# Weight products that stream their tokens in descending order: a hybrid decoder layer on one Trainium2 core

## The chip, the cores and the metric

The kernel runs on 1 core of one Trainium2 chip. The metric is the device time of one execution in microseconds (us), as the median of several runs. A profiled execution of the same kernel gives the trace.

## The reference, cut to what matters

One layer of a decoder for 256 tokens of 2048 features: a modulated RMSNorm, an input projection to three groups of heads (retention, RWKV-7, block-sparse attention), an output projection with a gated residual, then a second modulated norm and a gated MLP with a causal convolution, and a last norm.

```python
def conv_glu_ffn(h, w_up, conv_w, conv_b, w_down):
    S = h.shape[1]
    u = h @ w_up
    up = jnp.pad(u, ((0, 0), (CONV_WIDTH - 1, 0), (0, 0)))
    u = sum(conv_w[j] * up[:, j:j + S] for j in range(CONV_WIDTH)) + conv_b
    val, gate = jnp.split(u, 2, axis=-1)
    return (jax.nn.silu(gate) * val) @ w_down

def reference(x, c, w_in, w_out, ..., norm_final):
    c_act = jax.nn.silu(c)
    for l in range(DEPTH):
        mod = (c_act @ w_ada[l] + b_ada[l])[:, None, :]
        sh1, sc1, g1, sh2, sc2, g2 = jnp.split(mod, 6, axis=-1)
        h = rms_norm(x, norm_mix[l]) * (1.0 + sc1) + sh1
        x = x + g1 * hybrid_mixer(h, w_in[l], w_out[l], ...)
        h = rms_norm(x, norm_ffn[l]) * (1.0 + sc2) + sh2
        x = x + g2 * conv_glu_ffn(h, w_ffn_up[l], ffn_conv_w[l], ffn_conv_b[l], w_ffn_down[l])
    return rms_norm(x, norm_final)
```

The change touches the four large products with the weights: `h @ w_in`, `mixed @ w_out`, `h @ w_up` and the one with `w_down`.

## The kernel before

Activations lie with features on the 128 partitions and the 256 tokens along the free axis. A weight product takes a 128 x 128 block of weights as the stationary operand and a feature slice of 128 x 256 tokens as the moving one, and adds into a 128 x 256 piece of a PSUM bank; an output tile of 128 features is the sum over all feature slices `k`.

To keep fp32 accuracy, weights and activations are each split in a high and a low part of type fp32r (`hi`, `lo`), and three products are made for each block: high by high, high by low, low by high (L1192, L1193, L1194).

The weights stream from memory in blocks of 16 products, 1 MB, in an order that is written out ahead (`ORDER`). A block is turned into two chunks of eight: ScalarE makes the high part (`hi`, L458), VectorE the low part (`lo`, L459). `convert_until` runs `AHEAD` = 2 chunks ahead of TensorE. Among the blocks lie those of the modulation weights (`w_ada`), which VectorE multiplies and sums by itself (`raw`, L413). When one is known, `h_tile` makes one slice of the modulated input: `xn` (L439), `hhi` (L440), `hlo` (L441). Four slices share a tile.

The main loop goes over the chunks. For each of the eight products it opens a piece of a bank if the tile begins, picks the moving operands with `operands` (the tiles `hhi`/`hlo`, `mxhi`/`mxlo` or `ghi`/`glo`), and issues the three matmuls. In the input projection some tiles share a bank in pairs (`both`, tile name `pair`). For the first tiles of the up projection (`early`) the moving operand is `xghi`/`xglo`, 258 columns: 256 tokens and two columns of the shift. A tile whose sum is whole, or stops for a while, goes to `ready` with its piece of the bank and is evacuated by `evac_in`, `evac_out`, `evac_up` or `evac_down` on ScalarE or VectorE (L492, L494, L1032, L1099, L1115, L1133). After each chunk `run_tasks` issues a few steps of the heads, whose matmuls are plain fp32, such as the gate of the RWKV heads (`g`, L680).

Of the kernel before, what the change touches and what calls it, by code (L numbers as in the profile page):

```python
# [173 lines left out]
def trunk(tc, A):  # L174
# [25 lines left out]
    def nm(s):  # L200
        count[0] += 1
        return f"{s}{count[0]}"
# [86 lines left out]
    for f in range(4, NF):  # L289
        part = win[4 if f == 4 else cut[f - 5]:cut[f - 4]]  # L290
# [105 lines left out]
    for g in range(4):  # L396
        ps = psum.tile([128, 512], F32, tag="bg", name=nm("cb"), bufs=4)
# [50 lines left out]
    def convert_until(c):  # L448
        while len(chunks) <= c and pos[0] < len(stream_items):
            it = stream_items[pos[0]]  # L450
            raw = raws[pos[0]]
            if it[0] == "ada":
                ada_block(it[1], it[2], raw[0])
            else:
                half = half_of[0]
                hi, lo = (stream.tile([128, 8, 128], F32R, tag=n, name=nm(n), bufs=CONVB) for n in ("hi", "lo"))
                src = raw[half] if len(raw) == 2 else raw[0][:, 1024 * half:1024 * half + 1024]
                S.copy(flat(hi), src)  # L458
                V.tensor_tensor(flat(lo), src, flat(hi).bitcast(F32), op=OP.subtract)  # L459
                chunks.append((it[1], 16 * it[2] + 8 * half, hi, lo))  # L460
                half_of[0] = 1 - half
                if half_of[0]:
                    continue
            pos[0] += 1
            consumed[0] += 1
            pump()
# [528 lines left out]
    def run_tasks(n):  # L995

        for i in range(n):
            head = first_task[0]
            if head and alive[0] + head[1] <= 3 and (i % 2 == 0 and not hold - finished or not tasks):
                first_task[0] = step(head[0])  # L1000
                continue
            for i, (t, need) in enumerate(tasks):
                if alive[0] + need <= 3:
                    break
            else:
                if head and alive[0] + head[1] <= 3:
                    first_task[0] = step(head[0])
                continue
            tasks.pop(i)
            again = step(t)  # L1010
            if again:
                tasks.append(again)
# [132 lines left out]
    def operands(m, k):  # L1145
        src = H if m in ("in", "up") else MX if m == "out" else GT
        if m == "down":
            k = RANK[k]
        hi, lo = src[k // 4]
        return hi[:, k % 4], lo[:, k % 4]  # L1150
# [15 lines left out]
    for c in range(n_chunks):  # L1166
        convert_until(c + AHEAD)
        for f in hooks.pop(c, []):
            f()
        m, base, whi, wlo = chunks[c]  # L1170
        ready = []
        for j in range(8):
            t, k, first, last, part = ORDER[m][base + j]
            if first:
                spare = c >= first_up
                turn[0] += 1
                if m == "in" and k == 0 and t in S_TILES + W_TILES:

                    if t % 2 == 0:
                        tag, n = ("bg", 4) if t in S_TILES else ("mm", 3) if t != W_TILES[-2] else ("y", 1)  # L1180
                        pair[0] = psum.tile([128, 512], F32, tag=tag, name=nm("pair"), bufs=n)
                    both[t] = pair[0]
                    opened[t] = pair[0][:, T * (t % 2):T * (t % 2) + T]
                elif spare and turn[0] % 2:
                    opened[t] = psum.tile([128, 512], F32, tag="bg", name=nm("mm"), bufs=4)
                else:
                    opened[t] = psum.tile([128, 512], F32, tag="mm", name=nm("mm"), bufs=3)
            early = m == "up" and t % NP < EARLY and k < 4
            ps = opened[t][:, 0:T + 2] if early else opened[t][:, 0:T]
            hi, lo = (x[:, k] for x in XG) if early else operands(m, k)  # L1190
            two = t in both
            PE.matmul(ps, whi[:, j], hi, start=first and not (two and t % 2), stop=False, skip_group_check=two)  # L1192
            PE.matmul(ps, whi[:, j], lo, start=False, stop=False, skip_group_check=two)  # L1193
            PE.matmul(ps, wlo[:, j], hi, start=False, stop=last, skip_group_check=two)  # L1194
            if last:
                del opened[t]
                if not two:
                    ready.append((t, part, ps))
                elif t % 2:
                    ready.append((t - 1, part, both.pop(t)))  # L1200
                    del both[t - 1]
        for t, part, ps in ready:
            evac[m](t, part, ps)
        run_tasks(TASKS)
# [75 lines left out]
```

## Time and profile before

| what | value |
|---|---|
| time, median of 3 runs | 1283.11 us (1282.66 to 1283.84) |
| time of the profiled execution | 1284.61 us |
| span of the profiled execution | 1282.8 us |
| TensorE busy | 1242.3 us, 97% of the span |
| VectorE busy | 1031.6 us, 80% |
| ScalarE busy | 650.6 us, 51% |
| GpSimd busy | 39.9 us, 3% |
| moved from and to memory | 320.56 MB, 250 GB/s in the mean |

The span goes from the first to the last instruction of the trace; the time of the execution is 1.8 us longer. PE is TensorE's matmuls, PEld its weight loads, DVE VectorE, ACT ScalarE, POOL GpSimd. Matmuls are pipelined, so the record of one (some 280 ns) overlaps the next, and the pace is read from start to start.

### The profile page before, as it was taken

What the parts mean: (1) busy time and instruction counts of PE and PEld (TensorE: products, weight loads), DVE (VectorE), ACT (ScalarE), POOL (GpSimd) and SP (SyncE); (2) the same over time, 40 slices, a digit from 0 to 9 for tenths busy, and PEclk for the clock granted to TensorE, in tenths of its full rate; (3) what the DMA queues carried; (4) which work ended last, traced back from release to release, by engine and by line L of the source; (5) the groups of instructions that cost most, each with busy time, mean ns of one, the idle gap of its engine ahead of it and who ended that gap; (6) DMA issues with size and microseconds to landing.
All of it is one profiled execution on the core that took longest, in us unless ns stands there. A gap on an engine that the chain in (4) does not pass through costs nothing.

```text
span 1282.8 us, 25320 instructions
## 1 busy us (share of the span) xinstructions
PE 1242.3 (97%) x10524; PEld 1222.0 (95%) x10524; DVE 1031.6 (80%) x1606; ACT 650.6 (51%) x1043; POOL 39.9 (3%) x41
## 2 busy tenths in 40 slices
PE   5899999999999999999999999999999999999996
PEld 4799999999998999999999999999999999999995
DVE  7988989989988478999896999899866766666444
ACT  4455444665435333566555656666555544444441
POOL 0000000000000000500000000000000000000000
PEclk7999999999999999999999999999999999999998
DMA  9999987786636459867985566565655677777551
GB/s 388 349 360 344 341 311 268 290 294 209 232 104 235 155 204 363 319 233 259 350 307 200 197 213 208 184 225 194 220 205 198 230 263 254 285 254 281 207 197 66
DMA packets 49939, 320.56 MB, mean 250 GB/s; under 512 B 5536, under 2 KB 6048, under 8 KB 15776
## 3 DMA queue, kind: packets, MB, share of 16 engines
q1 hardware_dynamic: 48528, 315.10, 67.8%
q0 software_dynamic: 1008, 3.67, 0.8%
q8 instruction: 82, 1.34, 0.4%
q14 instruction: 33, 0.27, 0.1%
q10 hardware_dynamic: 288, 0.17, 0.0%
HBM read 316.83 MB, written 2.10 MB: 249 GB/s over the span
## 4 chain that ended last, share of the span: by engine, by line
PE 89%; DVE 7%; issue 2%; ACT 1%; DMA 0%; POOL 0%; DVEq 0%; ACTq 0%; POOLq 0%
PE mm L1192 26%; PE mm L1194 26%; PE mm L1193 26%; DVE raw L413 2%; DVE lo L459 2%; PE pair L1194 1%; PE pair L1192 1%; PE pair L1193 1%; PE xx L778 1%; PE u L915 1%; PE sp L923 1%; PE sp L937 1%; PE akv L788 1%; PE yps L917 0%; ACT hi L458 0%
## 5 line engine op out<-in xcount | busy, mean ns | idle before, releaser
L459 DVE TENSOR_TENSOR lo<-raw,hi 128x1024 fp32r<-128x1024 f32 x400 | 488.4, 1224 | 161.0 <-ACT hi L458 158.2
L458 ACT CAST hi<-raw 128x1024 fp32r<-128x1024 f32 x400 | 418.7, 1049 | 391.7 <-PE mm L1193 333.0
L1192 PE MATMUL mm<-hhi,hi 128*128 128x256 f32 x2016 | 560.2, 278 | 0.2
L1194 PE MATMUL mm<-hhi,lo 128*128 128x256 f32 x2016 | 559.4, 278 | 0.7 <-DVE lo L459 0.7
L1193 PE MATMUL mm<-hlo,hi 128*128 128x256 f32 x2016 | 559.5, 278 | 0.0
L1194 PEld LDWEIGHTS mm<-hhi,lo 128*128 128x128 f32 x2016 | 379.2, 188 | 1.7 <-DVE lo L459 1.3
L1192 PEld LDWEIGHTS mm<-hhi,hi 128*128 128x128 f32 x2016 | 379.1, 188 | 1.3 <-issue 0.3
L1193 PEld LDWEIGHTS mm<-hlo,hi 128*128 128x128 f32 x2016 | 378.8, 188 | 0.3
L413 DVE SCALAR_TENSOR_TENSOR raw<-raw,cb 128x2048 f32<-128x2048 f32 x96 | 221.3, 2305 | 10.4 <-DMA raw<-w_ada 9.6
L1192 PE MATMUL mm<-ghi,hi 128*128 128x256 f32 x704 | 194.8, 277 | 0.0
L1193 PE MATMUL mm<-glo,hi 128*128 128x256 f32 x704 | 194.8, 277 | 0.0
L1194 PE MATMUL mm<-ghi,lo 128*128 128x256 f32 x704 | 194.8, 277 | 0.0
L1192 PEld LDWEIGHTS mm<-ghi,hi 128*128 128x128 f32 x704 | 132.2, 188 | 0.0
L1194 PEld LDWEIGHTS mm<-ghi,lo 128*128 128x128 f32 x704 | 132.2, 188 | 0.0
L1193 PEld LDWEIGHTS mm<-glo,hi 128*128 128x128 f32 x704 | 132.2, 188 | 0.0
L1192 PE MATMUL mm<-mxhi,hi 128*128 128x256 f32 x256 | 73.9, 289 | 1.3 <-DVE x L1032 1.3
L1194 PE MATMUL mm<-mxhi,lo 128*128 128x256 f32 x256 | 72.1, 282 | 0.5 <-DVE lo L459 0.5
L1193 PE MATMUL mm<-mxlo,hi 128*128 128x256 f32 x256 | 72.3, 283 | 0.0
L1046 POOL TENSOR_TENSOR acc<-acc,nsq 128x256 f32<-128x256 f32 x28 | 34.0, 1213 | 808.4 <-ACT nsq L1045 808.2
L1192 PE MATMUL pair<-hhi,hi 128*128 128x256 f32 x160 | 45.0, 294 | 7.6 <-ACT hi L458 5.6
L1192 PEld LDWEIGHTS mm<-mxhi,hi 128*128 128x128 f32 x256 | 48.3, 188 | 3.2 <-DVE x L1032 1.2
L1194 PEld LDWEIGHTS mm<-mxhi,lo 128*128 128x128 f32 x256 | 48.5, 189 | 0.6 <-DVE lo L459 0.6
(292 smaller groups left out, 1301.5 us busy)
## 6 DMA issues: line engine op xcount, KB each, us to landing
raw<-w_ada SPq DMA_DIRECT2D x96, 1024.0 KB, 5.7
raw<-w_up SPq DMA_DIRECT2D x67, 1024.0 KB, 4.8
raw<-w_in SPq DMA_DIRECT2D x52, 1024.0 KB, 6.6
raw<-w_down SPq DMA_DIRECT2D x44, 1024.0 KB, 4.9
raw<-w_up SPq DMA_DIRECT2D x42, 512.0 KB, 8.1
raw<-w_out SPq DMA_DIRECT2D x18, 512.0 KB, 9.1
raw<-w_out SPq DMA_DIRECT2D x7, 1024.0 KB, 5.0
x<-xT SPq DMA_DIRECT2D x4, 512.0 KB, 5.4
```

What stands on the lines that cost most here:

```text
L413: V.scalar_tensor_tensor(raw, raw, 1.0, cb, op0=OP.mult, op1=OP.mult, accum_out=m)
L458: S.copy(flat(hi), src)
L459: V.tensor_tensor(flat(lo), src, flat(hi).bitcast(F32), op=OP.subtract)
L778: PE.matmul(ps[:, T * i:T * i + 128], L[pb, f, sl], At[pb, f, sl], start=True, stop=True)
L788: PE.matmul(ps[:, 128 * i + 64 * e:128 * i + 64 * e + 64], xv[:, e, 128 * i:128 * i + 128], vT[:, h, 64 * hd:64 * hd + 64], start=True, st ...
L915: PE.matmul(ups[pb, 128 * f:128 * f + 128], M1[:, f, ts], sb[:, f], start=True, stop=True)
L923: PE.matmul(sp[:, fs], kT[pb, h, fs], vT[pb, h, fs], start=(f == 0), stop=False, skip_group_check=True)
L937: PE.matmul(sp[:, fs], bT[pb, h, fs], U[pb, h, fs], start=False, stop=True, skip_group_check=True)
L1046: (V if t == NF - 1 else G).tensor_tensor(norm["acc"], norm["acc"], sq, op=OP.add)
L1192: PE.matmul(ps, whi[:, j], hi, start=first and not (two and t % 2), stop=False, skip_group_check=two)
L1193: PE.matmul(ps, whi[:, j], lo, start=False, stop=False, skip_group_check=two)
L1194: PE.matmul(ps, wlo[:, j], hi, start=False, stop=last, skip_group_check=two)
```

## The change

The moving operands `hi` and `lo` and the piece of the bank `ps` are all turned round along the tokens before the three matmuls, so that column 255 (257 for the early tiles) is read and written first and column 0 last. Each column of the result stays where it was. What is handed on to the evacuation is turned back. The weights are not touched.

```diff
@@ -1189,13 +1189,15 @@
             ps = opened[t][:, 0:T + 2] if early else opened[t][:, 0:T]
             hi, lo = (x[:, k] for x in XG) if early else operands(m, k)
             two = t in both
+
+            ps, hi, lo = (x[:, ::-1] for x in (ps, hi, lo))
             PE.matmul(ps, whi[:, j], hi, start=first and not (two and t % 2), stop=False, skip_group_check=two)
             PE.matmul(ps, whi[:, j], lo, start=False, stop=False, skip_group_check=two)
             PE.matmul(ps, wlo[:, j], hi, start=False, stop=last, skip_group_check=two)
             if last:
                 del opened[t]
                 if not two:
-                    ready.append((t, part, ps))
+                    ready.append((t, part, ps[:, ::-1]))
                 elif t % 2:
                     ready.append((t - 1, part, both.pop(t)))
                     del both[t - 1]
```

## Rows read from the trace of the kernel before

**Rows 1.** The page: busy time, 40 slices in tenths, chain that ended last.

```profile
span 1282.8 us, 25320 instructions
PE 1242.3 (97%) x10524; PEld 1222.0 (95%) x10524; DVE 1031.6 (80%) x1606; ACT 650.6 (51%) x1043; POOL 39.9 (3%) x41
...
PE   5899999999999999999999999999999999999996
...
PEclk7999999999999999999999999999999999999998
...
PE 89%; DVE 7%; issue 2%; ACT 1%; DMA 0%; POOL 0%; DVEq 0%; ACTq 0%; POOLq 0%
```

**Rows 2.** Table of stretches: length, busy time and instructions by engine, granted clock, DMA.

```profile
0.00:20.00 20.00, 6.68 (x36) 6.43 (x36) 11.60 (x27) 9.85 (x12) 0.20 (x4) 0.87 0.93 370
20.00:40.00 20.00, 15.86 (x107) 15.11 (x108) 17.76 (x23) 5.67 (x8) 0.00 (x0) 0.79 1.01 405
40.00:60.00 20.00, 16.28 (x127) 15.67 (x125) 18.55 (x23) 8.92 (x13) 0.00 (x0) 0.91 0.88 317
...
560.00:700.00 140.00, 140.00 (x1233) 140.00 (x1232) 121.14 (x148) 81.58 (x147) 0.00 (x0) 1.00 0.78 285
...
1260.00:1283.00 23.00, 10.01 (x81) 9.43 (x79) 8.76 (x20) 1.92 (x3) 0.00 (x0) 0.74 0.23 92
```

**Rows 3.** Table of stretches for tile mm: PE, PEld, DVE, ACT, clock, DMA.

```profile
560.00:1260.00 700.00, 700.00 (x6160) 700.00 (x6159) 55.72 (x123) 33.90 (x95) 1.00 0.66 233
```

**Rows 4.** Groups by line and shape, TensorE: busy us, mean ns, idle before.

```profile
L1192 PE MATMUL mm<-hhi,hi 128*128 128x256 f32 x2016 | 560.2, 278 | 0.2
...
L1192 PE MATMUL mm<-ghi,hi 128*128 128x256 f32 x704 | 194.8, 277 | 0.0
...
L1192 PE MATMUL mm<-mxhi,hi 128*128 128x256 f32 x256 | 73.9, 289 | 1.3 <-DVE x L1032 1.3
...
L1192 PE MATMUL pair<-hhi,hi 128*128 128x256 f32 x160 | 45.0, 294 | 7.6 <-ACT hi L458 5.6 <-ACT hhi L440 1.9
...
L1192 PE MATMUL mm<-xghi,hi 128*128 128x258 f32 x64 | 18.2, 285 | 0.0
```

**Rows 5.** Order of time, TensorE: first and last start of 25 products.

```profile
1000.20 0.28 PE L1192 MATMUL mm<-hhi,hi 128*128 128x256 f32 x1
...
1002.92 0.28 PE L1192 MATMUL mm<-hhi,hi 128*128 128x256 f32 x1
```

**Rows 6.** Order of time, 258-column products: first and last start of 16.

```profile
559.97 0.28 PE L1192 MATMUL mm<-xghi,hi 128*128 128x258 f32 x1
...
561.77 0.29 PE L1192 MATMUL mm<-xghi,hi 128*128 128x258 f32 x1
```

**Rows 7.** Order of time near the start: first and last start of 13 products.

```profile
25.68 0.42 PE L1194 MATMUL pair<-hhi,lo 128*128 128x256 f32 x1
...
28.24 0.35 PE L1193 MATMUL pair<-hlo,hi 128*128 128x256 f32 x1
```

**Rows 8.** Chain that ended last, in order of time: start, length, what.

```profile
32.17 2.22 DVE raw L413 x2
...
41.44 2.22 DVE raw L413 x2
...
246.89 1.73 PE g L680 x8
```

**Rows 9.** Groups by line and shape, VectorE: two multiplies over 512 elements.

```profile
L834 DVE TENSOR_TENSOR tmp<-xi,pr 128x512 f32<-128x512 f32 x1 | 1.0, 1043 | 0.0
L827 DVE TENSOR_TENSOR tmp<-ad,xi 128x512 f32<-128x512 f32 x1 | 0.7, 683 | 0.0
```

**Rows 10.** TensorE's waits: total us, times, longest.

```profile
PE pair L1192 <- ACT hhi L440: 1.9, 1, 1.9
```

**Rows 11.** ScalarE's waits: total us, times, longest.

```profile
ACT hi L458 <- PE mm L1193: 333.0, 246, 5.0
```

## The prediction

> **What bounds the kernel now.** I read the page first, then the table of stretches, the groups of matmuls by shape, the order of time on TensorE, the chain that ended last, and the waits.
>
> The page shows TensorE busy for 1242.3 of 1282.8 us, in every slice but the first two and the last at 90% or more, and the chain that ended last lies on TensorE for 89% of the span [rows 1]. A busy TensorE alone proves little, since each matmul's record (278 ns) overlaps the next. So the second view is the table of stretches: from 560 to 700 us the engine has no gap at all [rows 2], and from 560 to 1260 us 6160 records of the weight products fill 700.00 of 700.00 us, which is 113.6 ns for one [rows 3]. The idle time, 1282.8 - 1242.3 = 40.5 us, lies mostly in the first 60 us and the last 23 [rows 2], where transfers, the modulation blocks and the last norm are awaited.
>
> The third view says how many products there are. The first of the three matmul lines, L1192, has 2016 + 704 + 256 + 160 + 64 = 3200 of them [rows 4]; L1193 and L1194 run as often (one issue of each per step of the loop), so 9600 in all. The order of time gives the pace that a mean duration hides: from 1000.20 to 1002.92 us 24 products start in 2.72 us, one every 113.3 ns [rows 5]. [...] 9600 x 113.3 ns = 1088 us, 85% of the span. Nothing else is near it: the cast of the next weights on ScalarE waits 333.0 us in total for TensorE to give buffers back [rows 11].
>
> So what counts is the pace of one product. 1 ns on each is 9.6 us of the total. [...]
>
> **The change part by part.**
>
> *Instruction count.* Three matmuls a step before, three after, with the same shapes, types, start and stop flags. No weight load, transfer, wait or queue is moved in the text: 0 us. The weight operands are not turned round.
>
> *The reading of the moving operand.* 256 fp32 columns per product, from column 255 down to 0. No row of this trace has a descending operand, on any engine. [...]
>
> [...] VectorE shows that order can cost: two multiplies over 512 elements take 683 ns where the innermost step of both inputs is one element or a repeat, and 1043 ns where one of them jumps 16 elements each time [rows 9], a factor of 1.53. That factor on TensorE would be 60 ns a product, 576 us. But a descending read does not jump: each element is next to the one before. It is nearest to the one-element case, so I take 0, with 986 us kept as the upper end for the range.
>
> *The writing of the bank.* The products of a tile add into the same 256 (or 258) columns in the same order as each other, so the distance between two additions to one column remains a whole product. [...] I take 0 by the same reasoning: neighbours stay neighbours. [...] No row here decides.
>
> *The evacuation.* The tuple handed on is turned round again, so ScalarE and VectorE read the bank ascending as before; paired banks are passed whole. 0 us.
>
> *Waits.* The program's waits follow from which slices overlap. If a turned slice were taken for its whole tile, a first product would wait for the next h slice of that tile. In the starved stretch weight-and-modulation rounds come 41.44 - 32.17 = 9.27 us apart [rows 8], and the product's wait for hhi is 1.9 us today [rows 10]. Conversion runs two chunks ahead, one block, so the delay is one round, about 9 us, once. I take 0.
>
> The sum is 0 on the profiled execution's 1284.6 us (span 1282.8), which lies 1.5 us above the median of the three runs. The forecast is the median, 1283.1 us.
>
> **The rivals.**
>
> [...]
>
> [...]
>
> [...]
>
> 4. *Coarser waits (slower).* 1283 + 9 = 1292 us.
>
> [...]
>
> That the change does nothing the chip notices is the forecast itself.
>
> **How the numbers follow.** No change 0.55, half rate 0.24, fixed price 0.12, two records 0.03, coarser waits 0.02, faster 0.04. I give half rate that much because no row has a negative step, so 0 is argued from adjacency alone. The likeliest case's own range is 1280.5 to 1285.7 us. Up to the fixed price only 0.55 + 0.12 + 0.02 = 0.69 would be held, so the range has to reach over half rate: 1280 to 2275 us leaves out two records and faster, 0.07. Faster 0.04, within 0.2% 0.55, slower 0.24 + 0.12 + 0.03 + 0.02 = 0.41.
>
> **What would show it.** [...] The 258-column products should stay at 120.0 ns. The counts of L1192 to L1194, each 3200 here, would double if a product became two records. Should a wait be the cause instead, the pace would stay and TensorE's idle time in the first 60 us would grow. The evacuations on L494, L1032, L1099 and L1115 should keep their durations; if they lengthen, they read the bank descending after all. [...] The forecast is wrong if any of these steps shows a price, most of all one inside the stream, since nothing hides it.

## The result and the profile after

The changed kernel takes 1314.1 us (four runs, 1313.95 to 1317.37) beside 1283.5 us for the kernel before on the same chip: a ratio of 1.0246, 95% interval 1.0228 to 1.0263. It is slower by 31 us. The forecast was no change. A few executions of the kernel before, and of e7 and e12 below, took some 2% longer at the same granted clock (0.985 to 0.991 in all executions); no comparison uses them.

The page of the profiled execution, with the lines that answer to [rows 1]:

```profile
span 1312.4 us, 25327 instructions
PE 1272.6 (97%) x10524; PEld 1253.3 (95%) x10524; DVE 1034.1 (79%) x1606; ACT 649.7 (50%) x1043; POOL 40.1 (3%) x41
...
PEclk8899999999999999999999999999999999999998
...
PE 91%; DVE 6%; issue 1%; ACT 1%; DMA 0%; POOL 0%; DVEq 0%; ACTq 0%; POOLq 0%
```

TensorE has as many matmuls as before and is busy for 30 us more; its idle time, 1312.4 - 1272.6 = 39.8 us, is what it was (40.5). So the time went into the stream of products and into no wait. The order of time, as in [rows 5], first and last start of 22 products:

```profile
1000.30 0.28 PE L1194 MATMUL mm<-hhi,hi 128*128 128x256 f32 x1
...
1002.77 0.28 PE L1194 MATMUL mm<-hhi,hi 128*128 128x256 f32 x1
```

21 products in 2.47 us are 117.6 ns each, where [rows 5] gave 113.3. The table of stretches says the same of 400 us of the up projection, and something else of an earlier stretch (length, busy time and count of PE, PEld, DVE, ACT, POOL, clock, DMA). First the kernel before:

```profile
140.00:190.00 50.00, 50.00 (x427) 50.00 (x426) 44.73 (x60) 20.51 (x24) 0.00 (x0) 1.00 0.87 331
600.00:1000.00 400.00, 400.00 (x3532) 400.00 (x3531) 339.55 (x522) 236.54 (x351) 0.00 (x0) 1.00 0.65 227
```

and the changed one:

```profile
140.00:190.00 50.00, 50.00 (x426) 49.91 (x425) 44.97 (x60) 21.41 (x26) 0.00 (x0) 1.00 0.85 324
600.00:1000.00 400.00, 400.00 (x3399) 400.00 (x3398) 331.64 (x507) 228.30 (x343) 0.00 (x0) 1.00 0.63 220
```

From 600 to 1000 us a product takes 400 / 3532 = 113.3 ns before and 400 / 3399 = 117.7 ns after, 4.4 ns more, at a granted clock of 1.00 and with no gap in either. From 140 to 190 us, in the input projection, both kernels run at 117 ns: 427 and 426 products in 50 us. The kernel before thus had two paces, and in this execution this stretch of it had nothing to lose. That is not fixed. e15 below issues the same instructions up to the up projection; from 75 to 100 us, first the kernel before, then e15:

```profile
75.00:100.00 25.00, 25.00 (x223) 25.00 (x222) 21.15 (x25) 13.85 (x25) 0.00 (x0) 1.00 0.96 351
```

```profile
75.00:100.00 25.00, 25.00 (x214) 25.00 (x214) 20.38 (x24) 14.17 (x25) 0.00 (x0) 1.00 0.92 349
```

So in the input projection an ascending stream takes one pace or the other, and with the same instructions not always the same one. From 140 to 190 us e15 has 426 products and five other kernels that read ascending there (e2, e4, e10, e11, e12) have 441 to 444; what decides it is not shown. From 600 to 1000 us the profiled executions of all kernels that only read ascending (the kernel before and those five) have 3528 to 3532 products.

Where the time went is read from the first start of the up projection's `xghi` products and the first and last of the down projection's `ghi` products (group by tile: durations, first and last start in us). Before:

```profile
L1192 PE MATMUL mm<-xghi,hi x64: 277/283/371, 541.8 to 569.7; 128*128 128x258 f32 x64
...
L1192 PE MATMUL mm<-ghi,hi x704: 276/276/282, 1027.1 to 1267.7; 128*128 128x256 f32 x176
```

After:

```profile
L1194 PE MATMUL mm<-xghi,hi x64: 282/283/364, 545.6 to 573.5; 128*128 128x258 f32 x64
...
L1194 PE MATMUL mm<-ghi,hi x704: 279/279/283, 1048.7 to 1297.1; 128*128 128x256 f32 x176
```

All that lies ahead of the up projection lost 545.6 - 541.8 = 3.8 us, a figure that hangs on how much of this one execution of the kernel before ran at the slower pace (against e4, whose up projection began at 537.5 us, it would be 8.1). The up projection took 503.1 us for 485.3, 17.8 us more; the down projection 248.4 for 240.6, 7.8 us more. The sum, 29.4 us, is the span's difference of 29.6.

The wait of TensorE that answers to [rows 10] and the durations of the evacuations did not move (before, the two below took 417 and 477 ns):

```profile
PE pair L1194 <- ACT hhi L440: 1.9, 1, 1.9
```

```profile
L494 DVE TENSOR_TENSOR proj<-mm,proj 128x256 f32<-128x256 f32 x52 | 20.9, 418 | 4.2 <-PE mm L1196 4.0
L1032 DVE SCALAR_TENSOR_TENSOR x<-mm,mod_g,x 128x256 f32<-128x256 f32 x32 | 15.0, 477 | 13.0 <-PE mm L1196 12.8
```

### The profile page after: what moved, and what is told of

It is laid out like the page before. It is cut to its first block, busy times and chain, and to the rows that moved or that the text cites. A ratio compares the mean times of both kernels' runs of the same rounds, so it can differ in the third digit from the quotient of the medians.

```text
span 1312.4 us, 25327 instructions
## 1 busy us (share of the span) xinstructions
PE 1272.6 (97%) x10524; PEld 1253.3 (95%) x10524; DVE 1034.1 (79%) x1606; ACT 649.7 (50%) x1043; POOL 40.1 (3%) x41
## 4 chain that ended last, share of the span: by engine, by line
PE 91%; DVE 6%; issue 1%; ACT 1%; DMA 0%; POOL 0%; DVEq 0%; ACTq 0%; POOLq 0%
PE mm L1194 26%; PE mm L1195 26%; PE mm L1196 26%; DVE raw L413 1%; PE pair L1194 1%; DVE lo L459 1%; PE pair L1195 1%; PE pair L1196 1%; PE xx L778 1%; PE sp L923 1%; PE sp L937 1%; PE u L915 1%; PE akv L788 1%; PE xx L779 0%; ACT hi L458 0%
## 5 line engine op out<-in xcount | busy, mean ns | idle before, releaser
L1194 PE MATMUL mm<-hhi,hi 128*128 128x256 f32 x2016 | 569.5, 283 | 0.0
L1195 PE MATMUL mm<-hlo,hi 128*128 128x256 f32 x2016 | 568.8, 282 | 0.0
L1196 PE MATMUL mm<-ghi,lo 128*128 128x256 f32 x704 | 198.5, 282 | 0.0
L1195 PE MATMUL mm<-glo,hi 128*128 128x256 f32 x704 | 198.5, 282 | 0.0
```

## The experiments

Each kernel is read by its pace in the up projection from 600 to 1000 us, which is steadier than its time, and by its time. Times are medians of 2 runs (e1 to e6, e8, e9), 3 (e13), 6 to 8 (e7, e10 to e12) or a single run (e14, e15); those without a ratio are read beside 1283 us. Unless the text says otherwise an edit is made in the kernel before.

**e1 and e2: reading alone, writing alone.**

```diff
 e1:
+            hi, lo = (x[:, ::-1] for x in (hi, lo))
 e2:
+            ps = ps[:, ::-1]
...
+                    ready.append((t, part, ps[:, ::-1]))
```

> Only the moving operands are turned round; the bank is written ascending, so the tokens of each product come out in reverse order and the output is not the reference's. Theory A (the reading costs): as the full change, 117.8 ns from start to start in the up projection and 1314 us. Theory B (the writing of the bank costs): as before, 113.3 ns and 1283 us. Theory C (the place of the moving read against the weight load that runs beside it costs): as A, because the read decides that place, 117.8 ns and 1314 us.

> Only the bank is written descending; the moving operands are read ascending, so the tokens come out in reverse order and the output is not the reference's. Theory A (reading): as before, 113.3 ns in the up projection and 1283 us. Theory B (writing): 117.8 ns and 1314 us. Theory C (place of the read against the weight load): as before, 113.3 ns and 1283 us. If both halves cost something, e1 and e2 lie between and their extra times add up to 31 us.

The same stretch of e1, then of e2:

```profile
600.00:1000.00 400.00, 400.00 (x3399) 400.00 (x3398) 331.13 (x507) 228.60 (x343) 0.00 (x0) 1.00 0.62 219
```

```profile
600.00:1000.00 400.00, 400.00 (x3532) 400.00 (x3531) 339.15 (x521) 236.66 (x352) 0.00 (x0) 1.00 0.64 227
```

e1 took 1313.4 us with 3399 products, exactly the count of the full change; e2 took 1285.2 us with 3532, exactly that of the kernel before. The whole loss is in reading. Theory B fell: writing the bank from its last column to its first cost nothing here (400 / 3532 = 113.3 ns).

**e3 and e4: the weights moved by 256 bytes against the activations.**

```diff
-    stream.tile([128, 80], F32, name="pad")
+    stream.tile([128, 16], F32, name="pad")
```

> The changed kernel with the pad ahead of the weight tiles cut from 80 to 16 floats, so that weights lie 256 bytes lower and the moving tiles where they were. Theories A and B: 117.8 ns and 1314 us as without it. Theory C: another pace than 117.8 ns in the up projection, down to 113.3 ns and 1283 us if the new place is free of the conflict.

> The kernel before with the same pad cut from 80 to 16 floats. Theories A and B: 113.3 ns in the up projection and 1283 us as before. Theory C: another pace, towards 117.8 ns or above, and up to 1314 us, as the place of the ascending read against the weight load moves by 256 bytes.

e3 (this edit in the changed kernel) ran at 400 / 3398 = 117.7 ns and took 1315.0 us; e4 ran at 400 / 3532 = 113.3 ns and took 1283.2 us. Neither pace moved, which speaks against theory C at this distance.

**e5, e6 and e7: which part of the order costs.**

```diff
 e5:
+            hi, lo = (x if early else x.rearrange("p (a b) -> p a b", b=16)[:, :, ::-1] for x in (hi, lo))
 e6:
+            hi, lo = (x if early else x.rearrange("p (a b) -> p a b", b=16)[:, ::-1] for x in (hi, lo))
 e7:
+            hi, lo = (x if early else x.rearrange("p (a b) -> p a b", b=128)[:, ::-1] for x in (hi, lo))
```

> Read alone is changed: the 256 columns are taken in 16 groups of 16 (64 bytes) in ascending order, descending inside each group, so the tokens come out in another order and the output is not the reference's; the 258-column products stay as before. Theory D (only where the stream starts matters: any first column that is not the first word of 64 bytes costs): 117.8 ns and 1314 us, as the stream starts at column 15. Theory F (the order inside a line of 64 bytes matters): 117.8 ns or more. Theory E (going back to lower lines matters): 113.3 ns and 1283 us.

> The other half: the 16 groups of 16 columns are taken in descending order, ascending inside each group; the tokens come out in another order and the output is not the reference's. The stream starts at column 240, the first word of its 64 bytes. Theories D and F: 113.3 ns and 1283 us. Theory E (going back to lower lines): 117.8 ns or more and at least 1314 us; if each step back costs as a line does, 16 steps are dear and the pace is far above 120 ns.

> Read alone: columns 128 to 255 first, then 0 to 127, both ascending; the tokens come out in another order and the output is not the reference's. One step back in the whole stream, both halves start at the first word of a line. Theories D and F: 113.3 ns and 1283 us. Theory E: between 113.3 and 117.8 ns, as there is one step back and not 15.

The stretch of e5, e6 and e7, one fence each:

```profile
600.00:1000.00 400.00, 400.00 (x3013) 400.00 (x3012) 310.73 (x465) 211.93 (x341) 0.00 (x0) 1.00 0.59 204
```

```profile
600.00:1000.00 400.00, 400.00 (x3398) 400.00 (x3398) 330.93 (x508) 228.21 (x343) 0.00 (x0) 1.00 0.64 219
```

```profile
600.00:1000.00 400.00, 400.00 (x3532) 400.00 (x3531) 339.23 (x521) 236.83 (x352) 0.00 (x0) 1.00 0.65 227
```

e5: 132.8 ns, 1447.0 us, ratio 1.1273 (1.1237 to 1.1309). e6: 117.7 ns, 1315.4 us, 1.0247 (1.0215 to 1.0280). e7: 113.3 ns, 1284.8 us, 1.0011 (0.9987 to 1.0035). No theory had all three right. D fell with e6, which starts on the first word of 64 bytes and is as slow as the full change. E was right on e6, at the lower edge of its range on e7, and wrong on e5, which never leaves its 64 bytes downward and was the dearest. F was wrong on e6.

**e8: one product of three.**

```diff
-            PE.matmul(ps, wlo[:, j], hi, start=False, stop=last, skip_group_check=two)
+            PE.matmul(ps, wlo[:, j], hi[:, ::-1], start=False, stop=last, skip_group_check=two)
```

> Only the third product of each step (low weights by high activations) reads descending; it adds tokens in the wrong order, so the output is not the reference's. If every descending product has its own price of 4.4 ns: a third of the loss, 114.8 ns in the mean and 1293 us. If one descending product is enough to hold the whole stream at the slower of the two paces that the kernel before shows (113.3 and 117.8 ns): 117.8 ns and 1314 us.

```profile
600.00:1000.00 400.00, 400.00 (x3399) 400.00 (x3398) 331.25 (x508) 228.09 (x342) 0.00 (x0) 1.00 0.63 219
```

The whole loss again: 117.7 ns, 1314.1 us, ratio 1.0237 (1.0198 to 1.0277). Two of the three products still read ascending and no longer have their pace. A price of 4.4 ns at each descending product fell. The other expectation came out: one descending product in three holds the whole stream at a pace equal to the slower one of the kernel before.

**e9 and e10: shorter weight loads.** The first product of each step, and the last of a tile, keep all 128 weight columns.

```diff
-            PE.matmul(ps, whi[:, j], lo, start=False, stop=False, skip_group_check=two)
-            PE.matmul(ps, wlo[:, j], hi, start=False, stop=last, skip_group_check=two)
+            w = 128 if last else 64
+            PE.matmul(ps[0:64], whi[:, j, 0:64], lo, start=False, stop=False, skip_group_check=two)
+            PE.matmul(ps[0:w], wlo[:, j, 0:w], hi, start=False, stop=last, skip_group_check=two)
```

> The changed kernel, with the second product of each step and the third, but for the last one of a tile, loading only 64 of the 128 weight columns and writing 64 partitions; half of the features lack these terms, so the output is not the reference's. [...] Theory M (the moving read itself is slower): 117.8 ns and 1314 us stay.

> The kernel before with the same shorter weight loads, the control for e9; the output lacks the same terms. If 113.3 ns is set by the 256 moving columns: 113.3 ns and 1283 us. If it is set by the weight load: well below, towards 110 ns, and 1255 us.

e9 (made in the changed kernel): 400 / 3398 = 117.7 ns, 1313.6 us, ratio 1.0242 (1.0190 to 1.0294). e10: 400 / 3532 = 113.3 ns, 1280.8 us, 0.9981 (0.9966 to 0.9997). The shorter loads did take less time (some 134 ns for 188 in the records of both kernels), yet neither pace changed. That each product of the slower pace waits for its weight load is thereby out.

**e11 and e12: the place where an ascending stream starts.**

```diff
-CONST_PAD, SMALL_PAD = 32, 16
 e11:
+CONST_PAD, SMALL_PAD = 40, 16
 e12:
+CONST_PAD, SMALL_PAD = 48, 16
```

> The kernel before with 8 floats more of padding ahead of the activation tiles, so that each ascending stream starts 32 bytes into a line of 64 bytes. If any start off a line's first word is enough for the slower pace: 117.8 ns in the up projection and 1305 to 1314 us. If the direction is what counts: 113.3 ns and 1283 us.

> The kernel before with 16 floats more of padding, so that the streams start on a line of 64 bytes but 64 bytes into 512. If the four tiles of the down projection at 128 to 384 bytes into 512 run at 117 ns because of that place: 117 ns and some 1305 to 1314 us. If not: 113.3 ns and 1283 us.

e11: 400 / 3530 = 113.3 ns, 1285.0 us, 1.0014 (1.0002 to 1.0027). e12: 400 / 3528 = 113.4 ns, 1286.6 us, 1.0019 (1.0002 to 1.0036). Starting 32 bytes into 64, or 64 into 512, does not bring the slower pace.

**e13: one product in 24.**

```diff
-            PE.matmul(ps, wlo[:, j], hi, start=False, stop=last, skip_group_check=two)
+            PE.matmul(ps, wlo[:, j], hi if j else hi[:, ::-1], start=False, stop=last, skip_group_check=two)
```

> One product in 24 reads descending (the third of the first step of each chunk), which adds tokens in the wrong order, so the output is not the reference's. If the loss is a price of at most 13.3 ns at each descending product: 113.9 ns in the mean of the up projection, 1288 us. If one descending product puts the stream in the slower pace and it stays there: 117.8 ns, 1314 us.

```profile
600.00:1000.00 400.00, 400.00 (x3498) 400.00 (x3497) 336.31 (x519) 234.55 (x347) 0.00 (x0) 1.00 0.65 225
```

114.4 ns in the mean, 1294.3 us, ratio 1.0076 (1.0053 to 1.0099). Per descending product that is 24 x (114.35 - 113.25) = 26 ns, twice what was expected. The order of time shows where; the descending product is the one at 702.26:

```profile
702.26 0.28 PE L1194 MATMUL mm<-hhi,lo 128*128 128x256 f32 x1
702.38 0.28 PE L1192 MATMUL mm<-hhi,hi 128*128 128x256 f32 x1
702.50 0.29 PE L1193 MATMUL mm<-hlo,hi 128*128 128x256 f32 x1
702.62 0.28 PE L1194 MATMUL mm<-hhi,lo 128*128 128x256 f32 x1
702.74 0.28 PE L1192 MATMUL mm<-hhi,hi 128*128 128x256 f32 x1
702.85 0.28 PE L1193 MATMUL mm<-hlo,hi 128*128 128x256 f32 x1
```

It and the next three take 0.12 us each, 0.48 us for 0.453, and the pace is back. In the up projection a lone descending product slows the ascending ones behind it, and the stream does not stay slow.

In the down projection it can stay slow. First the whole of it, then 12 us of the first output tile in e13 and the same feature slices in the kernel before:

```profile
L1192 PE MATMUL mm<-ghi,hi x704: 276/281/284, 1028.9 to 1274.8; 128*128 128x256 f32 x176
```

```profile
1032.00:1044.00 12.00, 12.00 (x104) 12.00 (x104) 8.00 (x10) 5.51 (x7) 0.00 (x0) 1.00 0.76 283
```

```profile
1030.00:1042.00 12.00, 12.00 (x108) 12.00 (x107) 8.24 (x11) 5.83 (x7) 0.00 (x0) 1.00 0.77 290
```

It took 245.9 us for 240.6, or 60 ns for each of its 88 descending products. In the 12 us the ascending products between the descending ones, 23 in a row, run at the slower pace as well: 104 products for 108. So both expectations came out, each in another stretch.

**e14: descending inside 16 bytes.** As e5, with `b=4` for `b=16`.

> As e5, with groups of 4 columns (16 bytes) in place of 16: ascending groups, descending inside each; the tokens come out in another order and the output is not the reference's. e5 cost 132.9 ns, 19.6 ns over before for 16 groups. If each jump forward has that price (1.2 ns): 64 groups, 78 ns more, about 192 ns in the up projection and near 2000 us. [...]

```profile
600.00:1000.00 400.00, 400.00 (x3531) 400.00 (x3531) 339.59 (x521) 236.45 (x350) 0.00 (x0) 1.00 0.66 227
```

113.3 ns and 1285.3 us: no loss at all, with 63 jumps in a stream. The price of a jump fell. Counted from one piece of 16 bytes to the next, the full change steps down 63 times in a product, e5 48 times, e6 15 times, e7 once and e14 never. The three orders with many steps down lose time and the two others do not, but the loss does not grow with their number.

**e15: a stretch of 40 chunks.** Made in the changed kernel.

```diff
+            back = first_up + 60 <= c < first_up + 100
+            if back:
+                ps, hi, lo = (x[:, ::-1] for x in (ps, hi, lo))
...
+                    ready.append((t, part, ps[:, ::-1] if back else ps))
```

> Reading and writing descend in 40 chunks of the up projection alone (960 products), the rest is as before. If the slower pace lasts only as long as descending products come: 117.8 ns for 960 products and 113.3 ns after them, 1283 + 4 = 1287 us. If the stream stays in the slower pace once it is there: 117.8 ns to the end of the up projection, about 1295 us.

```profile
650.00:700.00 50.00, 50.00 (x443) 50.00 (x443) 37.53 (x47) 26.72 (x37) 0.00 (x0) 1.00 0.73 264
740.00:800.00 60.00, 60.00 (x511) 60.00 (x511) 53.94 (x94) 36.17 (x55) 0.00 (x0) 1.00 0.61 206
850.00:900.00 50.00, 50.00 (x443) 50.00 (x443) 45.92 (x83) 33.09 (x50) 0.00 (x0) 1.00 0.64 218
```

60 / 511 = 117.4 ns inside the stretch, 50 / 443 = 112.9 ns ahead of it and behind it (short windows count one product too many). Here the slower pace ends with the descending products. The time is 1289.5 us.

No version beat both kernels: e2, e7 and e14 equal the kernel before, and e10 leaves work out.

## Why the prediction was wrong

**The step that failed** is the reading of the moving operand: "It is nearest to the one-element case, so I take 0". It costs 4.4 ns a product in the up projection, where the kernel before ran at 113.3 ns (e1). The argument went by adjacency of elements, and adjacency does not decide: inside a piece of 16 bytes the order was free (e14, 113.3 ns), one step down in a product was free (e7, 113.3 ns), and 15 steps down, from each 64 bytes to the 64 below, brought the full loss (e6, 117.7 ns). The descending read holds the stream at 117.7 ns, a pace that ascending streams have too (117.1 ns from 140 to 190 us in the kernel before), but only in some stretches. VectorE's two rows [rows 9] had no descending read either, and as a scale they pointed to the wrong case.

**The likeliest case and its rivals.** No change, given 0.55, did not come; a fixed price per product, given 0.12, did. Its size was the author's estimate: what the 258-column products take more than the others, 120.0 - 113.3 = 6.7 ns [rows 5, 6], on each of 9600 products, 64 us. Measured were 4.4 ns in the up projection (three products together 13 ns), and 30 us in all, so both factors were too large. The second one because 113.3 ns was read in one stretch [rows 5] and multiplied over all: in the execution that was profiled the input and output projections ran at about 117 ns in much of their time already (50 us / 427 = 117.1 ns from 140 to 190 us, 20.73 us / 176 = 117.8 ns from 520 to 541 us) and lost 3.8 us. The first one because the 6.7 ns, which the author put down to two more columns, need not be theirs alone. In the trace of the kernel before, 256-column products that read tiles of the same kind (`gt_piece`; slices 0 to 7 of the down projection) have the slower pace as well, first and last start of 25:

```profile
1027.06 0.28 PE L1192 MATMUL mm<-ghi,hi 128*128 128x256 f32 x1
...
1029.87 0.28 PE L1192 MATMUL mm<-ghi,hi 128*128 128x256 f32 x1
```

That is 2.81 us / 24 = 117.1 ns, so some 4 of the 6.7 ns may belong to the tiles and not to the columns. "Fixed" was also not quite the word, as e8 and e13 show: one descending product in three costs 13 ns, three in three cost 13 ns, a lone one 26 ns in the up projection and 60 in the down projection. Half rate, given 0.24, did not happen. Its 986 us, the upper end that the reading kept for the range, were an estimate that gave a descending product the pace of the plain fp32 records of the gate, 1.73 us / 8 = 216 ns [rows 8]: (216 - 113.3) x 9600. No run shows that term: the full change ran at 117.7 ns and the dearest order, e5, at 132.8. Neither did two records come (the count stayed at 10524), nor coarser waits (the wait for hhi stayed at 1.9 us). That the range, 1280 to 2275 us, holds 1314.1 is owed to half rate, which it was stretched to cover.

**The steps that held.** The instruction count (10524 matmuls in both) and the evacuations (418 and 477 ns for 417 and 477) cost nothing, as said. The writing of the bank cost nothing (e2, 113.3 ns). That was luck, for it was argued in the same way as the reading, from neighbours. That the place of a stream's start costs nothing was the author's inference from the 258-column products [rows 6], and it held for 256 columns, 32 bytes into 64 (e11, 113.3 ns) and 64 into 512 (e12, 113.4 ns). The pace from start to start was the right test and answered at once: 117.7 ns for 113.3. That TensorE alone sets the end held: 29.4 us of lost pace are the 29.6 us of the span.

**What stays open.** Why steps down slow the stream is not shown, nor how many of them it takes between 1 and 15 in a product; groups between the 16 bytes of e14 and the 64 of e5, such as 32, were not run. e5, which in turns goes down by three pieces of 16 bytes, one at a time, and up by seven, costs 132.8 ns, more than a stream that only goes down; that is not explained. And the ascending kernel has the 117 ns pace without any descending read: for long stretches of the input projection, in some executions and not in others (427 products from 140 to 190 us in the kernel before, 441 to 444 in five others), and for slices 0 to 7 of the down projection (117.1 ns in the kernel before). Whether this is the same thing is open. The pace is the same, and in the down projection of e13 an ascending stream stays in it (104 products in 12 us for 108); but in the up projection of e13 the better pace came back within four products. That a tile's place plays a part is likely, since slices 0 to 7 lie in tiles of their own; e3, e4, e11 and e12 moved operands by 32 to 256 bytes only, and a larger distance is untested.

## What to carry to other kernels

Let moving operands be read with rising addresses: in this kernel the descending read took 117.7 ns a product for 113.3. Where an order has to be reversed, do it on the side of the bank (e2) or inside 16 bytes (e14), which both ran at 113.3 ns here. When a price is per product, read the pace in each stage from start to start before multiplying, and in more than one execution: the stretch that ran at 117 ns already lost nothing here (427 and 426 products from 140 to 190 us). A test on one product in many shows more than one on all, as neighbours may carry the price (in e13 the three products behind the descending one).

## What the runs showed of the hardware

- A descending fp32r read of 256 columns brings the stream from 113.3 to 117.7 ns a product in the up projection at a granted clock of 1.00, whether all products descend (e1) or each third one (e8).
- A lone descending product costs some 26 ns in the up projection, spread over itself and the three products behind it; in the down projection it costs 60 ns, as there up to 23 ascending products behind it stay slow (e13).
- Order inside 16 bytes was free (e14, 113.3 ns); 16 groups of 64 bytes, each read downward while the groups rise, ran at 132.8 ns a product (e5).
- Writing the bank downward was free (e2, 113.3 ns), and halving most weight loads (some 134 ns for 188) changed neither pace (117.7 ns in e9, 113.3 ns in e10).
- An ascending stream has the same two paces with the same shapes and the same granted clock, 1.00: in the kernel before 117 ns from 140 to 190 us and 113.3 ns from 600 to 1000 us. With the same instructions, 25 us of the input projection had 223 products in one execution and 214 in another (the kernel before and e15).
